# Gated delta rule on one Trainium2 core: solves of four heads, three chains at a time, and a new order of the products

## The chip, the cores and the metric

The kernel runs on one core of one Trainium2 chip. The metric is the time of one execution on the device in microseconds, as the median of three runs. A core has five engines that run side by side, each through its own list of instructions in order: TensorE (PE, matrix products), VectorE (DVE), ScalarE (ACT), GpSimd (POOL) and SyncE (SP), which here only issues DMA transfers. An instruction that needs another engine's result waits for a semaphore, and everything behind it in its engine's list waits with it.

## What is computed

One launch computes two residual blocks and a feed-forward part over 512 tokens of width 1024, batch 1, all in fp32. The first block adds two mixers, a gated delta rule of eight heads (width 128, chunks of 64 tokens in the reference) and a causal attention (MLA) of eight heads; then come a gated feed-forward part with a short convolution, and a second block (a state-space mixer beside a short convolution). The change touches only the delta rule:

```python
def gdn_chunked(q, k, v, g, beta):
    ...
    lmat = jnp.einsum("bhnid,bhnjd->bhnij", k_beta, k) * decay
    rhs = jnp.concatenate([v_beta, k_beta * jnp.exp(g)[..., None]], axis=-1)
    sol = lax.linalg.triangular_solve(lmat, rhs, left_side=True, lower=True, unit_diagonal=True)
    ...
    def step(state, inp):
        u_n, w_n, qd_n, kd_n, a_n, gl_n = inp
        v_new = u_n - jnp.einsum("bhck,bhkv->bhcv", w_n, state)
        o = jnp.einsum("bhck,bhkv->bhcv", qd_n, state) + jnp.einsum("bhij,bhjv->bhiv", a_n, v_new)
        state = state * gl_n[..., None, None] + jnp.einsum("bhck,bhcv->bhkv", kd_n, v_new)
        return state, o
    s0 = jnp.zeros((b, h, dk, dv), dtype=f32)
    _, o = lax.scan(step, s0, xs)
```

A unit lower triangular matrix is inverted for each chunk and head, and then a state of 128 x 128 runs through the chunks of a head, one after the other.

## The kernel before

The program is written by a generator in Python. Its bulk is a long row of linears: for each, eight blocks of weights of 128 x 128 are multiplied with activations of 512 tokens. An fp32 product is made of three fast ones (hi by hi, hi by lo, lo by hi), where `hi` is a rounded copy and `lo` the rest. The weights lie in memory in the order in which they are used, in chunks of eight blocks (512 KB). SP loads a chunk into one of two `raw` tiles (`NRAW`), ACT writes its `hi`, and DVE or POOL its `lo`, each into one of three tiles (`NHL`). A linear that belongs to the delta rule or to the attention is followed by work on its outcome.

That work is split into small tasks, Python generators that yield what they need next. `Emit.drive` (line 466) asks every running task for its next piece, and a planner (`Timeline`, with a cost for each instruction) tells which of them can go first; that one's instructions are written out. The main task is the row of linears, and it goes through `GDN_ORDER` (lines 31 to 36), a table written by hand; `order` (line 103) packs the weights by the same table. `kq` stands for the k and q of a head, `vg` for its v and output gate, `brb` and `bra` for the two gates of the block, `low`, `att`, `wv` and `ya` for the attention and the projections of both mixers. `LIMIT` (line 225) says how many tasks of one class may run at once, and `room()` counts free tiles of a common pool of 72 (`NG`), which are given back when nothing in Python refers to them any more. Since every instruction is issued by one helper, all rows of the profile read L243, and tiles tell them apart.

The tasks of a head:

- `t_gdn_a` (class a, two at once) normalises k and q, makes the matrices `ln` (the triangular one, four chunks of 128 tokens) and `at`, and sends the 32 x 32 blocks on the diagonal of `ln` to DRAM (`ldram`). After every second head it starts a solve.
- `t_solve` (class solve, one at once) loads the blocks of `NSOLVE` heads (line 1961) as `sl`, one block in each of 16 partitions a head, and inverts them in `sx`, in 31 steps of a multiplication into `st` and an addition into `sx`. For every four steps `idle` picks DVE or POOL by what the planner takes for their load. The inverses go to DRAM (`xdram`).
- `t_gdn_b` (class b, two at once) loads the inverses of its head as `X`, turns v, and completes the inverses of 128 x 128 with four groups of small products of 64 rows; `yodd`, one of two tiles, chosen by whether the head is odd, is an operand of the second. Then it runs the chain over four chunks: `gr` (from the state `gst`), `gvn` (from the inverse `Y`), and the next `gst`. Each is a product on PE and one instruction on DVE that reads it. Last come a norm and the gate.

```python
        for j0 in range(0, 31, 4):
            eng = self.idle(4000, 2000, POOL_BIAS)
```

Names that stand in rows: `mm` and `pt` are the results of products in PSUM (`mm` those of linears), `v` a convolution over the outcome of a linear (also for q and k, under their names), `rq_u` a step of an inverse square root.

Of the kernel before, what the change touches and what calls it, by code (L numbers as in the profile page):

```python
# [27 lines left out]


START = ["ab", ("k", 0), ("q", 0), ("k", 1)]  # L30
GDN_ORDER = [("kq", 3), ("vg", 0), ("brb", 0), ("kq", 4), ("brb", 1), ("vg", 1), ("brb", 2), ("vg", 2), ("brb",
             3), ("brb", 4), ("brb", 5), ("vg", 3), ("kq", 5), ("brb", 6), ("kq", 6), ("vg", 4), ("kq", 7),
             ("brb", 7), ("vg", 5), ("vg", 6), ("low",), ("vg", 7), ("bra", 0), ("wv", 0), ("bra", 1), ("bra",
             2), ("att", 0), ("att", 1), ("bra", 3), ("bra", 4), ("bra", 5), ("bra", 6), ("bra", 7), ("ya", 0),
             ("att", 2), ("ya", 1), ("att", 3), ("ya", 2), ("att", 4), ("wv", 1), ("ya", 3), ("att", 5), ("ya",
             4), ("att", 6), ("ya", 5), ("att", 7), ("ya", 6), ("ya", 7)]
PAIR_FFN = 3
FOLD_FFN = 3
# [64 lines left out]
def order():  # L103
# [5 lines left out]
    o = [START] + one([("q", 1), ("k", 2), ("q", 2)])  # L109
    for item in GDN_ORDER:  # L110
        if item[0] == "kq":
# [110 lines left out]
NHL = 3  # L222
AHEAD = 2
ROOM = {"kq": 5, "vg": 8, "att": 6, "wv": 5}
LIMIT = {"a": 2, "b": 2, "att": 2, "ssd": 2, "solve": 1, "E": 1, "pv": 1}


LAT = {"DVE": 33, "ACT": 33, "PE": 53, "POOL": 78, "SP": 60}
# [165 lines left out]
class Emit:  # L394
# [47 lines left out]
    def spawn(self, gen, cls=None):  # L442
        t = dict(gen=gen, cls=cls, need=None)
        if cls is not None and sum(x["cls"] == cls for x in self.tasks) >= LIMIT[cls]:
            self.waiting.setdefault(cls, []).append(t)
# [353 lines left out]
    def setup(self):  # L799
        nc, a = self.nc, self.a  # L800
        self.params = self.const.tile([128, NPARAM], F32, name="params")
        self.sqc = sq = self.const.tile([128, 5 * 128], F32, name="sqc")
        v = [sq[:, 128 * i:128 * i + 128] for i in range(5)]
        self.ident, self.ones, self.upper, low32, neg = v
        self.diag32 = low32[0:64, 0:64]
        self.yodd = []
        for i in range(2):
            t = self.const.tile([64, 256], F32, name=f"yodd{i}")
            nc.gpsimd.memset(t, 0.0)
            self.yodd.append(t)  # L810
        self.neg = neg

        self.rq, self.nk, self.bk = (self.const.tile([128, 32], F32, name=n) for n in ("rq", "nk", "bk"))
        self.ldram = self.dr.tile([8, NC, 4, 32, 32], F32, name="ldram")
        self.xdram = self.dr.tile([8, NC, 4, 32, 32], F32, name="xdram")
        one = self.s(1, "one", bufs=1)
        nc.gpsimd.memset(one, 1.0)
        nc.scalar.activation(one, one, AF.Silu)

        z = self.g(BF16, "warm")  # L820
        nc.vector.memset(z, 0.0)
        p = self.pt()
        for _ in range(NWARM):
            self.MM(p, z[:, 0:128], z, start=True, stop=True)
        self.hd, self.E = {}, {}
        self.oa, self.ob = {}, {}
# [121 lines left out]
    def t_gdn_a(self, h, kq):  # L948
        nc = self.nc
        hs = slice(4 * h, 4 * h + 4)  # L950
        yield self.flag("gates")

        yield lambda: "k" in kq
        k = kq["k"]
        yield [k]
        ss = self.s(8, "ss")
        pk = self.transpose4(k)
        junk = self.g(name="junk")
        yield [pk]
        for c in range(NC):  # L960
            nc.scalar.activation(junk[:, self.cc(c)], pk[:, self.cc(c)], AF.Square, accum_out=ss[:, c:c + 1])
        yield lambda: "q" in kq
        q = kq["q"]
        yield [q]
        pq = self.transpose4(q)
        yield [pq]
        for c in range(NC):
            nc.scalar.activation(junk[:, self.cc(c)], pq[:, self.cc(c)], AF.Square, accum_out=ss[:, 4 + c:5 + c])
        yield [ss]
        nc.vector.tensor_scalar(ss, ss, EPS, None, ALU.add)  # L970
        r = yield from self.rsqrt(ss, 8, "rkq")
        col = self.s(8, "kcol")
        nc.vector.tensor_tensor(col[:, 0:4], self.kdec[:, hs], r[:, 0:4], ALU.mult)
        del junk
        kt = self.g(name="ktok")
        nc.vector.tensor_tensor(self.v4(kt), self.v4(pk), self.colbc(col[:, 0:4]), ALU.mult)
        nc.vector.tensor_copy(self.rq[:, hs], r[:, 4:8])
        nc.vector.tensor_tensor(self.nk[:, hs], ss[:, 0:4], r[:, 0:4], ALU.mult)
        nc.vector.tensor_tensor(self.bk[:, hs], self.cmp[:, 64 + 4 * h:68 + 4 * h], r[:, 0:4], ALU.mult)
        nc.vector.scalar_tensor_tensor(col[:, 4:8], self.bk[:, hs], -1.0, r[:, 0:4], ALU.mult, ALU.mult)  # L980
        yield lambda: h in self.E
        e = self.E.pop(h)
        egb = self.rowload(self.grow[1, h])
        yield [e]
        at = self.g(name="at")
        ln = self.g(name="ln")
        for t, x, f in ((ln, k, col[:, 4:8]), (at, q, r[:, 0:4])):
            p = self.mm4(k, x)
            yield [p]
            for c in range(NC):  # L990
                nc.vector.scalar_tensor_tensor(t[:, self.cc(c)], p[:, self.cc(c)], f[:, c:c + 1], e[:, self.cc(c)],
                                               ALU.mult, ALU.mult)
        yield [ln]
        for b in range(4):
            nc.sync.dma_start(
                self.ldram[h, :, b].rearrange("c j i -> j c i"),
                self.v4(ln)[32 * b:32 * b + 32, :, 32 * b:32 * b + 32])
        yield [egb]
        nc.gpsimd.tensor_tensor(q, q, egb, ALU.mult)
        self.hd[h] = dict(kd=kt, kT=k, ln=ln, at=at, qd=q)  # L1000
        if h % NSOLVE == NSOLVE - 1:
            self.spawn(self.t_solve(h - NSOLVE + 1, NSOLVE), "solve")

    def t_solve(self, h0, n):

# [26 lines left out]
    def t_gdn_b(self, h, vg):  # L1032
# [3 lines left out]
        d = self.hd.pop(h)  # L1036
# [3 lines left out]
        X = self.g(name="X")  # L1040
        nc.gpsimd.memset(X, 0.0)

        ln = d["ln"]
        T = self.g(name="T")
        lnodd = T[:, 256:512].rearrange("p (c i) -> p c i", c=NC)
        nc.scalar.copy(T[:, 256:512].rearrange("p (c a i) -> p c a i", c=NC, a=2),
# [4 lines left out]
                self.v4(X)[32 * b:32 * b + 32, :, 32 * b:32 * b + 32],  # L1051
                self.xdram[h, :, b].rearrange("c i j -> i c j"))
        yield lambda: "v" in vg
        v = vg["v"]
        yield [v]
        p = self.transpose4(v)
        vb = self.g(name="vb")
        yield [p]
        nc.vector.tensor_tensor(self.v4(vb), self.v4(p), self.colbc(self.nk[:, hs]), ALU.mult)
# [10 lines left out]
        p = self.pt()  # L1070
        for c in range(NC):
            self.MM(half(p)[0:64, c], lnodd[:, c], xe[:, c, :, 0], start=True, stop=True)
        Yo = self.yodd[h % 2]
        for a in range(2):
            nc.vector.transpose(q4(Yo)[side(a), :, a], xe[odd(a), :, a, 1])
        yield [p]
# [3 lines left out]
        p = self.pt()  # L1080
        for c in range(NC):
            self.MM(half(p)[0:64, c], half(Yo)[:, c], half(T)[0:64, c], start=True, stop=True)
        yield [p]
        for a in range(2):
            nc.vector.tensor_copy(xe[odd(a), :, a, 0], q4(p)[side(a), :, a])
        for a in range(2):
            o, i = slice(64 * a + 32, 64 * a + 64), slice(64 * a, 64 * a + 32)
# [4 lines left out]
        for c in range(NC):  # L1092
            self.MM(half(p)[64:128, c], self.v4(ln)[0:64, c, 64:128], self.v4(X)[0:64, c, 0:64],
                    start=True, stop=True)
        yield [p]
        nc.scalar.copy(T[64:128, :256], p[64:128, :256])
        yield [T, Y]
# [49 lines left out]
        a = self.s(4, "soa")  # L1147
# [192 lines left out]
    def block1(self):  # L1340
# [95 lines left out]
        yield from self.unfold()  # L1436
        for item in GDN_ORDER:
            if item[0] == "kq":
# [184 lines left out]
    def t_dt(self, w, xh, fold):  # L1623
# [15 lines left out]
        p = self.pt()  # L1639
        for c in range(NC):  # L1640
            self.nc.tensor.transpose(p[:, 32 * c:32 * c + 32], z[0:32, self.cc(c)], self.ident[0:32, 0:32])
        pt = self.s(64, "dtr", bufs=1)
        yield [p]
        nc.vector.tensor_reduce(pt, p[:, 0:128].rearrange("p (c j q) -> p c q j", c=NC, j=2), AX.X, ALU.add)
        pt = self.v4(pt)
# [312 lines left out]
        yield from self.block2()  # L1958


NSOLVE = 2
SLACK = 0
POOL_BIAS = 2200
NWARM = 10
# [44 lines left out]
```

## Time and profile before

| what | value |
|---|---|
| median of three runs | 1508.0 us (1507.99 to 1508.04) |
| the profiled execution | 1510.79 us |
| its span, first to last instruction | 1508.8 us |
| PE busy | 1461.3 us, 97% |
| DVE, ACT, POOL busy | 887.0, 662.9, 553.5 us |
| mean granted clock of TensorE | 0.985 |

The page of the profile gives busy times over the whole program. The delta rule stands in its first third, so the windows of the trace (busy time of each engine in a stretch) and the chain of instructions in that third say more than the page's shares. In a row, a duration in brackets with an arrow is the idle time of the engine ahead of that instruction, and whose work ended it.

### The profile page before, as it was taken

How to read it: one execution, taken by the hardware profiler on the slowest of the kernel's cores; microseconds unless marked ns; L12 is line 12 of the kernel's file. 1: busy time of each engine (PE TensorE's matmuls, PEld its weight loads, DVE VectorE, ACT ScalarE, POOL GpSimd, SP SyncE). 2: the span in 40 equal slices, each digit the busy share in tenths (PEclk: the TensorE clock that was granted, in tenths of full speed). 3: DMA queues.
4: the chain of work that ended last, by engine and by line, in shares of the span. 5: the costliest groups of instructions: out<-in, count | busy, mean ns of one | idle time of the engine just before them, and what ended most of it. 6: DMA issues, size and time to landing. Idle time of an engine off the chain costs nothing.

```text
span 1508.8 us, 19107 instructions
## 1 busy us (share of the span) xinstructions
PE 1461.3 (97%) x7084; PEld 1196.9 (79%) x7084; DVE 887.0 (59%) x1801; ACT 662.9 (44%) x1124; POOL 553.5 (37%) x365
## 2 busy tenths in 40 slices
PE   8699989999999999999999999999999999999998
PEld 6588777787888888888888888888787787878877
DVE  7979978888854555348542044434975574360073
ACT  4565344433455655345442144344454453442342
POOL 0211124314143333442655455544115434543421
PEclk9899999999999999999999999999999999999999
DMA  5144413232231223442333332332233434422322
GB/s 185 53 121 138 122 46 93 79 97 64 70 95 60 63 78 105 147 126 84 111 99 98 97 97 89 95 103 94 70 95 114 122 98 119 125 87 89 95 94 98
DMA packets 56957, 147.63 MB, mean 98 GB/s; under 512 B 15072, under 2 KB 15648, under 8 KB 56864
## 3 DMA queue, kind: packets, MB, share of 16 engines
q1 hardware_dynamic: 56864, 146.42, 32.0%
q8 instruction: 55, 0.90, 0.2%
q14 instruction: 38, 0.31, 0.1%
HBM read 139.48 MB, written 5.34 MB: 96 GB/s over the span
## 4 chain that ended last, share of the span: by engine, by line
PE 59%; DVE 3%; issue 0%; ACT 0%; POOL 0%; DMA 0%; DVEq 0%; ACTq 0%
PE mm L243 56%; PE pt L243 3%; DVE lo L243 1%; DVE mix L243 0%; DVE xr L243 0%; DVE xbc L243 0%; DVE ysc L243 0%; DMA raw<-wstream 0%; DVE xn L243 0%; ACT hi L243 0%; DVE ms_a L243 0%; DVE sh L243 0%; POOL sh L243 0%; POOL xn L243 0%; POOL rs L243 0%
## 5 line engine op out<-in xcount | busy, mean ns | idle before, releaser
L243 PE MATMUL mm<-hi,hi 128*128 128x512 f32 (+2 forms) x1872 | 748.5, 400 | 6.5 <-ACT hi L243 4.4
L243 PE MATMUL mm<-lo,hi 128*128 128x512 f32 (+2 forms) x1872 | 731.9, 391 | 10.7 <-DVE lo L243 10.7
L243 PE MATMUL mm<-hi,lo 128*128 128x512 f32 (+2 forms) x1872 | 730.6, 391 | 3.7 <-DVE lo L243 3.7
L243 POOL TENSOR_TENSOR lo<-raw,hi 128x1024 fp32r<-128x1024 f32 x149 | 358.2, 2404 | 542.2 <-ACT hi L243 500.5
L243 PEld LDWEIGHTS mm<-lo,hi 128*128 128x128 f32 x1872 | 356.3, 190 | 79.0 <-DVE lo L243 13.1
L243 PEld LDWEIGHTS mm<-hi,lo 128*128 128x128 f32 x1872 | 355.2, 190 | 79.8 <-DVE lo L243 5.1
L243 PEld LDWEIGHTS mm<-hi,hi 128*128 128x128 f32 x1872 | 355.6, 190 | 78.8 <-ACT hi L243 8.5
L243 ACT ACTIVATE hi<-raw 128x1024 fp32r<-128x1024 f32 (+1 forms) x230 | 242.3, 1053 | 250.9 <-PE mm L243 175.6
L243 DVE TENSOR_TENSOR lo<-raw,hi 128x1024 fp32r<-128x1024 f32 (+1 forms) x81 | 100.2, 1238 | 2.8 <-ACT hi L243 2.7
L243 DVE TENSOR_TENSOR sq<-sq,sq 128x512 f32<-128x512 f32 x43 | 32.7, 773 | 93.1 <-ACT sq L243 92.9
L243 DVE TENSOR_TENSOR xr<-xr,mm 128x512 f32<-128x512 f32 x24 | 16.5, 687 | 97.5 <-PE mm L243 97.5
L243 DVE TENSOR_TENSOR lo<-fu,hi 128x512 fp32r<-128x512 f32 x22 | 44.6, 2027 | 42.0 <-ACT hi L243 42.0
L243 DVE SCALAR_TENSOR_TENSOR fu<-mm,params,fu 128x510 f32<-128x510 f32 (+1 forms) x38 | 28.5, 749 | 61.5 <-ACT fu L243 60.9
L243 ACT ACT_TABLE_LOAD x43 | 55.2, 1283 | 11.1 <-DVE k L243 2.2
L243 POOL TENSOR_TENSOR st<-sl,sx 32x112 f32<-32x112 f32 (+15 forms) x47 | 24.0, 512 | 80.2 <-issue 34.2
L243 POOL TENSOR_TENSOR fu<-fg,fu 128x512 f32<-128x512 f32 x22 | 30.0, 1361 | 42.4 <-DVE fu L243 42.4
L243 POOL TENSOR_TENSOR q<-q,row 128x512 f32<-128x512 f32 x8 | 10.9, 1365 | 78.7 <-PE pt L243 73.9
L243 DVE TENSOR_TENSOR lo<-scz,hi 128x512 fp32r<-128x512 f32 x8 | 15.8, 1969 | 32.7 <-ACT hi L243 32.7
L243 DVE TENSOR_TENSOR lo<-pt,hi 128x512 fp32r<-128x512 f32 (+3 forms) x32 | 15.7, 489 | 31.4 <-ACT hi L243 31.3
L243 DVE TENSOR_TENSOR st<-sl,sx 32x247 f32<-32x247 f32 (+15 forms) x77 | 29.9, 388 | 4.8 <-POOL sx L243 2.6
L243 DVE SCALAR_TENSOR_TENSOR fg<-mm,params,fg 128x510 f32<-128x510 f32 (+1 forms) x38 | 28.2, 743 | 6.2 <-ACT fg L243 5.5
L243 ACT ACTIVATE fg<-fg 128x512 f32<-128x512 f32 x22 | 13.9, 632 | 40.4 <-DVE fg L243 40.3
(314 smaller groups left out, 1578.8 us busy)
## 6 DMA issues: line engine op xcount, KB each, us to landing
raw<-wstream SPq DMA_DIRECT2D x228, 512.0 KB, 3.6
row<-grow_d SPq DMA_DIRECT2D x16, 256.0 KB, 4.2
row<-crow_d SPq DMA_DIRECT2D x16, 256.0 KB, 4.5
x<-xT SPq DMA_DIRECT2D x8, 256.0 KB, 6.5
sbd<-gate SPq DMA_DIRECT2D x8, 256.0 KB, 2.0
sb<-sbd SPq DMA_DIRECT2D x8, 256.0 KB, 3.8
xr<-xT SPq DMA_DIRECT2D x8, 256.0 KB, 3.8
Ce<-crow_d SPq DMA_DIRECT2D x16, 128.0 KB, 4.7
```

The source lines that it names most:

```text
L243: return f(*args, **kw)
```

## The change

Solves are made of four heads at a time on 64 partitions: two solves of 31 steps in place of four. A solve starts when all its heads have sent their blocks. Three chains may run at once, each with a `yodd` tile of its own, taken from a list and given back. A head's `ln` and `v` are dropped from the dictionaries that held them, so that their tiles come free once they are used. A tile of the second block shares the buffer of another (`gyb`). The table of the linears is new: it starts with a gate (`brb` 0) and the v of head 0, and the heads' k and q come earlier against their v.

```diff
@@ -28,11 +28,11 @@
-GDN_ORDER = [("kq", 3), ("vg", 0), ("brb", 0), ("kq", 4), ("brb", 1), ("vg", 1), ("brb", 2), ("vg", 2), ("brb",
...
+GDN_ORDER = [("brb", 0), ("vg", 0), ("kq", 3), ("brb", 1), ("brb", 2), ("kq", 4), ("brb", 3), ("brb", 4), ("brb",
...
@@ -222,7 +222,7 @@
 ROOM = {"kq": 5, "vg": 8, "att": 6, "wv": 5}
-LIMIT = {"a": 2, "b": 2, "att": 2, "ssd": 2, "solve": 1, "E": 1, "pv": 1}
+LIMIT = {"a": 2, "b": 3, "att": 2, "ssd": 2, "solve": 1, "E": 1, "pv": 1}
@@ -804,7 +804,7 @@
         self.yodd = []
-        for i in range(2):
+        for i in range(LIMIT["b"]):
             t = self.const.tile([64, 256], F32, name=f"yodd{i}")
@@ -998,8 +998,10 @@
         self.hd[h] = dict(kd=kt, kT=k, ln=ln, at=at, qd=q)
-        if h % NSOLVE == NSOLVE - 1:
-            self.spawn(self.t_solve(h - NSOLVE + 1, NSOLVE), "solve")
+        self.flags.add(("L", h))
+        h0 = h - h % NSOLVE
+        if all(("L", i) in self.flags for i in range(h0, h0 + NSOLVE)):
+            self.spawn(self.t_solve(h0, NSOLVE), "solve")
@@ -1040,7 +1042,7 @@
-        ln = d["ln"]
+        ln = d.pop("ln")
         T = self.g(name="T")
@@ -1051,9 +1053,10 @@
         yield lambda: "v" in vg
-        v = vg["v"]
+        v = vg.pop("v")
         yield [v]
         p = self.transpose4(v)
+        del v
         vb = self.g(name="vb")
@@ -1070,7 +1073,7 @@
             self.MM(half(p)[0:64, c], lnodd[:, c], xe[:, c, :, 0], start=True, stop=True)
-        Yo = self.yodd[h % 2]
+        Yo = self.yodd.pop(0)
         for a in range(2):
@@ -1080,6 +1083,7 @@
             self.MM(half(p)[0:64, c], half(Yo)[:, c], half(T)[0:64, c], start=True, stop=True)
+        self.yodd.append(Yo)
         yield [p]
@@ -1092,6 +1096,7 @@
                     start=True, stop=True)
+        del ln
         yield [p]
@@ -1639,7 +1644,7 @@
             self.nc.tensor.transpose(p[:, 32 * c:32 * c + 32], z[0:32, self.cc(c)], self.ident[0:32, 0:32])
-        pt = self.s(64, "dtr", bufs=1)
+        pt = self.s(64, "gyb", bufs=1)
         yield [p]
@@ -1958,7 +1963,7 @@
-NSOLVE = 2
+NSOLVE = 4
 SLACK = 0
```

What it does to the lists of the engines, at three places. On DVE, where the first two chains begin (`st` and `sx` are steps of a solve, `gvn` and `gst` of the chains), the list before reads:

```order
L243 TENSOR_TENSOR st_1598<-sl_1519,sx_1520 32x256
L243 TENSOR_TENSOR sx_1520<-sx_1520,st_1598 32x16x16
L243 TENSOR_SCALAR gvn_1801<-pt_1799,bk 128x128
L243 TENSOR_SCALAR gvn_1804<-pt_1802,bk 128x128
...
L243 TENSOR_TENSOR lo_1843<-raw_1822,hi_1829 128x1024
L243 TENSOR_TENSOR st_1598<-sl_1519,sx_1520 32x255
L243 TENSOR_TENSOR sx_1520<-sx_1520,st_1598 32x15x17
...
L243 COPY gst_1850<-pt_1848 128x128
```

and after the change:

```order
L243 COPY Y_1706<-pt_1793 64x4x64
L243 TENSOR_SCALAR rkq_1779<-rq_t_1778 128x8
L243 TENSOR_TENSOR rq_u_1781<-rkq_1779 128x8
L243 TENSOR_TENSOR rq_u_1781<-rq_u_1781,rq_h_1780 128x8
L243 SCALAR_TENSOR_TENSOR rkq_1779<-rq_u_1781,rkq_1779 128x8
L243 TENSOR_SCALAR gvn_1808<-pt_1806,bk 128x128
L243 TENSOR_SCALAR gvn_1813<-pt_1811,bk 128x128
...
L243 COPY gst_1831<-pt_1829 128x128
L243 COPY gst_1835<-pt_1833 128x128
```

Before, the steps of the second solve (heads 2 and 3) stand between the steps of the chains of heads 0 and 1; now none does, since heads 0 to 3 have one solve that ends ahead of the chains. In their place stand the norms of the next heads' k and q.

On PE, with the change, where three chains run (heads 4 to 6; `mm` is a linear):

```order
L243 MATMUL pt_3316<-Y_3231,T_3176 64x64 x4
L243 MATMUL pt_3321<-gvn_3303,ktok_1631 128x128
L243 MATMUL pt_3324<-vb_3168,Y_3216 128x128
L243 MATMUL mm_3210<-hi_583,hi_3076 128x512
L243 MATMUL mm_3210<-lo_588,hi_3076 128x512
L243 MATMUL mm_3210<-hi_583,lo_3086 128x512
L243 MATMUL pt_3333<-gvn_3303,at_1639 128x128
L243 MATMUL pt_3336<-gvn_3326,ktok_1854 128x128
L243 MATMUL pt_3339<-vb_3187,Y_3231 128x128
L243 MATMUL pt_3344<-gst_3323,k_1230 128x128
```

Products of three heads stand between those of one linear; before, two heads were the most.

On SP, with the change, after the first solve:

```order
L243 DMA xdram<-sx_1203 64x1024
L243 DMA X_1612<-xdram 32x4x32 x4
L243 DMA row_1637<-grow_d 128x512
L243 DMA X_1647<-xdram 32x4x32 x4
L243 DMA ldram<-ln_1640 32x4x32 x4
L243 DMA row_1697<-grow_d 128x512
L243 DMA raw_1700<-wstream 128x1024
...
L243 DMA ldram<-ln_1863 32x4x32 x4
L243 DMA X_1955<-xdram 32x4x32 x4
L243 DMA raw_1964<-wstream 128x1024
```

The load of the weights `raw_1700` stands behind the store of the inverses, eight loads of inverses and the four stores of head 4's `ln`; `raw_1964` behind those of one head more.

## Rows read from the trace of the kernel before

**Rows 1.** The page's busy times (busy us, share, instructions).

```profile
PE 1461.3 (97%) x7084; PEld 1196.9 (79%) x7084; DVE 887.0 (59%) x1801; ACT 662.9 (44%) x1124; POOL 553.5 (37%) x365
```

**Rows 2.** Windows: start:end, length, busy PE PEld DVE ACT POOL, clock, DMA share, GB/s.

```profile
180.00:285.00 105.00, 94.20 (x543) 78.02 (x542) 85.19 (x257) 39.90 (x118) 41.66 (x71) 0.93 0.26 78
285.00:420.00 135.00, 132.16 (x751) 108.06 (x750) 114.77 (x312) 54.35 (x130) 30.92 (x28) 1.00 0.25 75
```

**Rows 3.** Timeline of PE, 173 to 200: start, us, operation, [idle before, releaser].

```profile
174.63 0.67 PE L243 MATMUL pt<-T,yodd 64*64 64x64 f32 x8
193.51 0.60 PE L243 MATMUL pt<-gvn,at 128*128 128x128 f32 x4
199.34 0.77 PE L243 MATMUL pt<-gst,k 128*128 128x128 f32 x2 [5.23 <-DVE gst L243]
```

**Rows 4.** Timeline of DVE, 173 to 200.

```profile
173.93 0.42 DVE L243 TENSOR_TENSOR T<-pt,sqc 64x256 f32<-64x256 f32 x1
188.23 0.40 DVE L243 TENSOR_TENSOR st<-sl,sx 32x247 f32<-32x247 f32 x1
191.67 0.59 DVE L243 TENSOR_SCALAR gvn<-pt,bk 128x128 f32<-128x128 f32 x2
195.53 0.40 DVE L243 TENSOR_TENSOR st<-sl,sx 32x255 f32<-32x255 f32 x1
198.93 0.47 DVE L243 COPY gst<-pt 128x128 f32<-128x128 f32 x2
```

**Rows 5.** Timeline of PE, 234 to 245.

```profile
238.63 1.11 PE L243 MATMUL pt<-T,yodd 64*64 64x64 f32 x8 [2.48 <-DVE T L243]
```

**Rows 6.** Windows of 5 us, columns as in rows 2.

```profile
200.00:205.00 5.00, 5.00 (x19) 4.19 (x19) 1.00 (x4) 1.44 (x2) 3.74 (x7) 0.55 0.02 5
240.00:245.00 5.00, 5.00 (x18) 3.56 (x17) 3.96 (x12) 0.28 (x1) 1.10 (x5) 0.50 0.57 166
```

**Rows 7.** Groups, 100 to 420: out<-in, shapes, count | busy, mean ns | idle.

```profile
L243 DVE TENSOR_TENSOR st<-sl,sx 32x247 f32<-32x247 f32 (+15 forms) x77 | 29.9, 388 | 4.8 <-POOL sx L243 2.6
L243 DVE TENSOR_TENSOR sx<-sx,st 32x247 f32<-32x247 f32 (+15 forms) x77 | 26.0, 338 | 2.7
L243 POOL TENSOR_TENSOR sx<-sx,st 32x112 f32<-32x112 f32 (+15 forms) x47 | 28.0, 595 | 3.7
L243 POOL TENSOR_TENSOR st<-sl,sx 32x112 f32<-32x112 f32 (+15 forms) x47 | 24.0, 512 | 80.2 <-issue 34.2 <-DVE rkq L243 29.1 <-DMA sl<-ldram 7.3
```

**Rows 8.** More groups of DVE, 100 to 420.

```profile
L243 DVE TENSOR_TENSOR lo<-raw,hi 128x1024 fp32r<-128x1024 f32 x31 | 38.2, 1233 | 0.0
L243 DVE SCALAR_TENSOR_TENSOR v<-mm,params,v 128x509 f32<-128x509 f32 (+2 forms) x21 | 15.6, 744 | 0.5
L243 DVE TENSOR_SCALAR gvn<-pt,bk 128x128 f32<-128x128 f32 x32 | 10.9, 343 | 5.2 <-PE pt L243 5.1
L243 DVE TENSOR_TENSOR rq_u<-rq_u,rq_h 128x4 f32<-128x4 f32 (+1 forms) x50 | 10.1, 204 | 1.1
```

**Rows 9.** The chain that ended last: start, us, engine, tile, instructions.

```profile
681.55 353.64 PE mm L243 x1560
1035.19 0.87 PE pt L243 x8
```

**Rows 10.** Timeline of PE, 270 to 283.

```profile
270.76 1.06 PE L243 MATMUL pt<-k 128*128 128x128 f32 x8
271.65 0.39 PE L243 MATMUL pt<-gst,k 128*128 128x128 f32 x2
```

**Rows 11.** Timeline of POOL and DVE, 358.5 to 362.5.

```profile
359.54 2.37 POOL L243 TENSOR_TENSOR lo<-raw,hi 128x1024 fp32r<-128x1024 f32 x1 [1.83 <-ACT hi L243]
359.60 2.35 DVE L243 TENSOR_SCALAR ms_a<-cs 128x4 f32<-128x4 f32 x1
```

**Rows 12.** SP's waits, 100 to 420 (us, times, longest); the page's landing times.

```profile
SPq L243 <- DVE ln L243: 13.7, 2, 8.2
raw<-wstream SPq DMA_DIRECT2D x228, 512.0 KB, 3.6
```

More of the change, by code (lines that the diff above doesn't have):

```diff
@@ L30 @@
 START = ["ab", ("k", 0), ("q", 0), ("k", 1)]
-GDN_ORDER = [("kq", 3), ("vg", 0), ("brb", 0), ("kq", 4), ("brb", 1), ("vg", 1), ("brb", 2), ("vg", 2), ("brb",
[L32 to L35, printed above, removed]
+GDN_ORDER = [("brb", 0), ("vg", 0), ("kq", 3), ("brb", 1), ("brb", 2), ("kq", 4), ("brb", 3), ("brb", 4), ("brb",
+             5), ("vg", 1), ("kq", 5), ("brb", 6), ("vg", 2), ("kq", 6), ("kq", 7), ("vg", 3), ("bra", 0),
+             ("brb", 7), ("vg", 4), ("vg", 5), ("vg", 6), ("low",), ("bra", 1), ("bra", 2), ("vg", 7), ("bra",
+             3), ("att", 0), ("wv", 0), ("att", 1), ("bra", 4), ("bra", 5), ("bra", 6), ("bra", 7), ("ya", 0),
+             ("att", 2), ("ya", 1), ("att", 3), ("wv", 1), ("ya", 2), ("att", 4), ("ya", 3), ("att", 5), ("ya",
              4), ("att", 6), ("ya", 5), ("att", 7), ("ya", 6), ("ya", 7)]
```

## The prediction

> **What bounds the kernel now.** I read the page's busy times first: PE is busy for 1461.3 us [rows 1], and DVE, the next, for 887.0. The change takes nothing from PE (6620 instructions in its list before and after, the same products in another order), so it can gain only what PE stands idle or runs slowly. Next come the windows of the stretch that the change reorders. In 180 to 285 PE is busy for 94.2 of 105 us, in 285 to 420 for 132.16 of 135 [rows 2]: it is idle for 10.8 + 2.8 = 13.6 us. In the first of these windows DVE is busy for 85.19 us, and the clock that TensorE was granted is 0.93. The timeline then tells where the idle time is: the longest wait is one of 5.23 us for `gst`, the first state of a chain [rows 3], the next one of 2.48 us for `T` in a later head [rows 5]. Behind each the granted clock falls, to 0.55 and 0.50 in five microseconds [rows 6], that is, for part of that time it stood on the lower of its levels, 1.2 GHz in place of 2.4. The cost is 0.45 x 5 + 0.5 x 5 = 4.75 us of PE's time. So the stretch loses 13.6 + 4.75 = 18.35 us, and that is the most that a better order can give back.
>
> **Why PE waits there.** From the end of the row `T` of head 1, at 173.93 + 0.41, to the first `gst`'s successor on PE at 199.34 DVE works 25.0 us without a gap; PE has products from 174.63 to 194.11, 19.5 us, and then nothing that does not need DVE [rows 3, 4]. 25.0 less 19.5 is 5.5, the wait. Of the 58 rows of DVE in it, counted from `T`, 32 are steps of the solve of heads 2 and 3. Sixteen of them run from 188.23 to 191.67 and from 195.53 to 198.93, 6.84 us [rows 4], straight ahead of `gvn` and of `gst`; the others by the means, (388 + 338) / 2 = 363 ns [rows 7], 5.8 us; together 12.6 us. The wait is thus made by a solve that DVE does between the steps of two chains.
>
> **The change, part by part.**
>
> Solves of four heads. A step on 64 partitions in place of 32 has as many elements in each partition; I take its time as unchanged, since the bound from above, twice the time, would need DVE to go by partitions, and a convolution of 128 partitions and 509 elements takes 744 ns, a solve's step of 32 partitions and at most 256 takes 388 on the mean [rows 7, 8]. In the list DVE has 54 + 54 steps in place of 77 + 77, POOL 8 + 8 in place of 47 + 47. On DVE that takes away 23 x (0.388 + 0.338) = 16.7 us; on POOL 39 pairs of 0.51 + 0.60 us by the means [rows 7], 43 us, which nobody waited for there. Half of the 124 pairs are gone altogether. What hides the 16.7 us of DVE now is PE's own work wherever DVE isn't late; so it counts only where PE waits.
>
> The first two chains. In the list after the change no step of a solve stands between their steps, but the solve's end comes later against the heads, and other rows have taken the place. From the convolutions of the next k to the `gr` of the second chunk the list of DVE has 81 rows: 6 convolutions, 6 more of 512 elements, 29 of at most 8 elements, 2 `lo`, 38 of 128 or 256. By the means that is 12 x 0.744 + 29 x 0.204 + 2 x 1.233 + 38 x 0.343 = 8.9 + 5.9 + 2.5 + 13.0 = 30.3 us [rows 8]. Means count some time twice, since instructions overlap at their ends: the 26 rows of before without the solve would make 4 x 1.233 + 3 x 0.744 + 19 x 0.343 = 13.7, and took 25.4 - 12.6 = 12.8, a share of 0.935. So I take 28.3 us. PE has, between the same two points, 53 products of linears at 353.64 / 1560 = 0.227, 16 transposes at 0.87 / 8 = 0.11 [rows 9], 24 products of 128 x 128 at (271.65 - 270.76) / 4 = 0.22 [rows 10] and 32 of 64 rows at 0.67 / 4 = 0.17 [rows 3]: 12.0 + 1.8 + 5.3 + 5.4 = 24.5 us. PE is short by 28.3 - 24.5 = 3.8 us, which I take as the wait in place of 5.23. From below it is nothing, if the planner's list runs as it thinks; from above 30.3 - 24.5 = 5.8, the means as they are.
>
> Three chains at once. Where heads 4 to 6 run, the list has 67 rows of DVE, some 23 us by the same prices, against 48 products of linears and as many of the chains, 28 us. DVE is not late there. Before, two chains leave less of other work between a product of a chain and the next; a third fills it. The price of the third `yodd` is one memset at the start, beside loads; the taking and giving back of these tiles and of `ln` and `v` issues nothing. The rename in the second block has no instruction.
>
> The other waits. Without the two longest 13.6 - 5.23 - 2.48 = 5.9 us are left in small pieces, each for a row that DVE does late. With 16.7 us less on DVE I take half, 2.9 us; all of it and nothing are the bounds. The 2.48 us I take as gone: the place in the order where they stood no longer exists; if it stays, it costs 2.5 and another 2.5 of clock.
>
> The clock. After 5.23 and 2.48 us of waiting it was granted at about half for five microseconds [rows 6]. A wait of 3.8 us in one piece would cost some 2.4, in short pieces perhaps nothing; I take half of the 2.5, 1.25. By the section "HAM oscillation" of the Trainium skill's page "TensorE: Matmul & The Clock Gate", pauses of PE between bursts of products bring the slow clock back again and again; the two rows agree that a pause is followed by it. By that rule alone, with each pause punished, the term would be 2.5, and the sum 1.25 more.
>
> SP. The loads of weights stand behind more transfers than before. A load lands in 3.6 us [rows 12], and both halves need at most 2 x 1.233 more [rows 8]: 6.1 us. Between the time at which `raw_1700` may be written and its first product PE has 48 products of linears (10.9 us) and by the same prices 11.8 us of the heads' own: 22.7 us. Less 6.1 and the two landings of the inverses' way through DRAM, 7.2, that leaves 9.4 us. I cost it at nothing.
>
> Sum: 3.8 + 2.9 + 1.25 = 8.0 us of loss in place of 18.35, a gain of 10.4. The profiled execution took 1510.8 us, 2.8 above the median of the three runs, and becomes 1500.4; the median becomes 1508.0 - 10.4 = **1497.6**.
>
> **The rivals.**
>
> *All waits go* (chance 0.12). The loss is nothing, the gain 18.35, the time 1489.6. For it speaks that DVE is also slowed by what POOL does: a row on four elements took 2.35 us beside a `lo` of POOL of 2.37 that had begun just before it [rows 11], where such a row takes 0.2 [rows 8]. With 43 us less of two-operand work on POOL such holds become rarer, and the planner, which knows none of them, is nearer to the truth. Against it: the 149 `lo` of POOL all stay, and DVE's row sum of the first chains is above PE's. The Trainium skill, "SBUF — State Buffer", section "SBUF: two separate sides", states that DVE and GpSimd share a pair of ports as a lock that one holds for a whole instruction; the row agrees.
>
> *Three chains bind each other* (0.12). A chain has its DVE row between any two of its products. With three at once 30 such rows of `gvn`, `gr` and `gst` (ten in each) at 0.343 [rows 8] could each stand ahead of a product that another chain needs: 10.3 us, the time 1497.6 + 10.3 = 1507.9, no change. Against it: PE has more work there than DVE, 28 against 23 us.
>
> *The weights come late* (0.08), the one on the other side. SP waits in order: the four stores of a `ln` wait for DVE, and `raw_1700` stands behind them, `raw_1964` behind the next. Before, SP waited up to 8.2 us for a `ln` [rows 12]. It decides when SP is held for over 9.4 us there. Two such waits, 16.4 us, at each of the two places make PE wait 7.0 us and cost 2.25 of clock: 18.5 us, the time 1516.1. Against it: before, no wait of PE in this stretch was for weights behind such a row.
>
> **How the numbers follow.** My forecast has 0.68. Its own range is from 1508.0 - 18.35 + 2.9 = 1492.5 (no wait in the first chains, no clock) to 1497.6 + 2.0 + 3.0 + 1.25 = 1503.9 (5.8 us there, all small waits, the whole clock term). With the first rival, 0.80 lie from 1489.6 to 1503.9; since prices are uncertain by a microsecond or two, and the second rival may come at part of its strength, I give 1488 to 1506. A measurement tells 0.2%, 3 us, from no change. Faster than 1505.0: forecast and first rival, 0.80. Within 3 us: the second rival, 0.12. Slower: the third, 0.08.
>
> **What would show it.** Right: 54 steps of each kind on DVE between 100 and 420, with about the same means, on 64 partitions; no step of a solve in the 25 us ahead of the first `gst`; PE's longest wait below 4 us and for a `gr`, `gvn` or `gst`; idle time of PE in the stretch at 6 to 7 us, and at most one window of 5 us with a clock near 0.5. The rest of the program, from the end of the attention on, the same to a microsecond. Wrong: a wait of PE for `hi` or `lo` behind an SP that waits for `ln`, steps of 64 partitions that take much longer than 0.36 us, waits for `gvn` and `gst` many and short where three chains run, or a changed time after 420.

## The result

The kernel after the change took 1485.1 us (median of four runs, 1484.6 to 1488.2) against 1508.0 of the kernel before: 0.985 of its time, 95% interval 0.9835 to 0.9869. That is 22.9 us less where 10.4 were forecast, and 2.9 us below the range. The sign was right, the size was not. The profiled execution took 1485.2 us with a span of 1483.2, so 25.6 us of span are gone; that of before stood 2.8 us above its median, that of after only 0.1.

The page's busy times after the change, which answer to [rows 1]:

```profile
PE 1449.1 (98%) x7084; PEld 1191.0 (80%) x7084; DVE 864.5 (58%) x1755; ACT 655.1 (44%) x1118; POOL 503.9 (34%) x284
```

PE has the same 7084 records and is busy for 12.2 us less, and idle for 1483.2 - 1449.1 = 34.1 us in place of 47.5, 13.4 less. Where the idle time went is seen in the windows, with the columns of [rows 2]; the third stretch, which the prediction did not look at, is shown for both kernels, after first:

```profile
180.00:285.00 105.00, 104.53 (x628) 86.68 (x627) 86.55 (x260) 46.58 (x131) 16.86 (x21) 1.00 0.31 94
285.00:420.00 135.00, 133.76 (x770) 111.22 (x769) 108.79 (x305) 59.33 (x134) 19.14 (x10) 1.00 0.25 74
420.00:600.00 180.00, 180.00 (x910) 153.22 (x909) 91.57 (x213) 98.55 (x198) 69.98 (x34) 1.00 0.30 90
```

```profile
420.00:600.00 180.00, 177.84 (x902) 150.13 (x901) 96.94 (x224) 104.65 (x215) 67.45 (x33) 1.00 0.27 83
```

In the three stretches PE is idle for 0.5, 1.2 and 0 us; before it was 10.8, 2.8 and 2.2. The granted clock is at its upper level in all three. Ahead of them nothing is gained: after the change PE is idle for 1.2 us between 100 and 180, where it was never idle before, and in the first 100 us it is idle for 0.9 us less, at a mean clock of 0.86 in place of 0.90.

PE's largest waits between 100 and 600 after the change (us, times, longest):

```profile
PE pt L243 <- DVE X L243: 0.9, 2, 0.6
PE pt L243 <- POOL q L243: 0.8, 1, 0.8
PE pt L243 <- ACT k L243: 0.4, 1, 0.4
PE pt L243 <- DVE gst L243: 0.3, 1, 0.3
```

No wait for a chain's `gvn` or `gr` is left, and one of 0.3 us for `gst`, where 5.23 stood in [rows 3]. From 600 on the program is as before with one exception. In the second block PE waits for a tile `dtz` as before, but in the kernel before the clock fell behind that wait, and after the change it did not (the wait and a window of 5 us, before, then after):

```profile
1080.70 0.43 PE L243 MATMUL pt<-sqc,dtz 32*128 32x32 f32 x4 [2.27 <-DVE dtz L243]
1080.00:1085.00 5.00, 4.30 (x14) 3.41 (x15) 4.93 (x8) 1.35 (x2) 0.00 (x0) 0.67 0.00 0
```

```profile
1056.30 0.43 PE L243 MATMUL pt<-sqc,dtz 32*128 32x32 f32 x4 [2.25 <-DVE dtz L243]
1055.00:1060.00 5.00, 3.70 (x18) 3.06 (x19) 4.93 (x8) 0.76 (x2) 0.00 (x0) 1.00 0.01 2
```

That is some 1.6 us of the 25.6, and it may be part of the 2.8 us by which the profiled execution of before stands above its median. The one edit in the second block, the shared buffer, does not decide it: the wait is 2.25 to 2.27 us long in the profiles of both kernels and of all twelve experiments below, and the clock falls behind it in ten of the fourteen. Of the four without the fall, two share that buffer (after, e12) and two do not (e8, e10).

The solves are what the list said. The groups of DVE, 100 to 420, after the change, which answer to [rows 7], with one size of step by its own shape, and that size before:

```profile
L243 DVE TENSOR_TENSOR st<-sl,sx 64x135 f32<-64x135 f32 (+15 forms) x54 | 23.2, 429 | 5.2 <-POOL sx L243 3.8
L243 DVE TENSOR_TENSOR sx<-sx,st 64x135 f32<-64x135 f32 (+15 forms) x54 | 18.9, 350 | 1.9
...
L243 DVE TENSOR_TENSOR st<-sl,sx 64x252 f32<-64x252 f32 x4 | 1.7, 414 | 0.1
```

```profile
L243 DVE TENSOR_TENSOR st<-sl,sx 32x252 f32<-32x252 f32 x6 | 2.5, 409 | 0.2
```

54 steps of each kind, and one on 64 partitions takes 414 ns where one on 32 takes 409: twice the heads at the same price. DVE has 13.8 us less of them than before (42.1 in place of 55.9), where the prediction took 16.7 by the means.

### The profile page after: what moved, and what is told of

Its sections match the earlier page's. It is cut to its first block, busy times and chain, and to the rows that moved or that the text cites. A ratio compares the mean times of both kernels' runs of the same rounds, so it can differ in the third digit from the quotient of the medians.

```text
span 1483.2 us, 18958 instructions
## 1 busy us (share of the span) xinstructions
PE 1449.1 (98%) x7084; PEld 1191.0 (80%) x7084; DVE 864.5 (58%) x1755; ACT 655.1 (44%) x1118; POOL 503.9 (34%) x284
## 4 chain that ended last, share of the span: by engine, by line
PE 85%; DVE 10%; DMA 2%; issue 1%; POOL 1%; ACT 1%; SPq 0%; DVEq 0%; POOLq 0%; ACTq 0%
PE mm L243 76%; PE pt L243 9%; DVE lo L243 3%; DVE st L243 1%; DVE sx L243 1%; DVE k L243 0%; DVE q L243 0%; SPq L243 0%; DVE rq_u L243 0%; DVE mix L243 0%; DMA raw<-wstream 0%; DVE v L243 0%; DVE xr L243 0%; DVE x L243 0%; ACT hi L243 0%
## 5 line engine op out<-in xcount | busy, mean ns | idle before, releaser
L243 POOL TENSOR_TENSOR q<-q,row 128x512 f32<-128x512 f32 x8 | 10.4, 1294 | 157.9 <-PE pt L243 92.5
L243 ACT ACT_TABLE_LOAD x37 | 47.5, 1283 | 8.3 <-DVE xbc L243 2.6
L243 DVE TENSOR_TENSOR lo<-pt,hi 128x512 fp32r<-128x512 f32 (+3 forms) x32 | 15.6, 489 | 28.9 <-ACT hi L243 28.8
L243 DVE SCALAR_TENSOR_TENSOR fg<-mm,params,fg 128x510 f32<-128x510 f32 (+1 forms) x38 | 28.3, 744 | 6.2 <-ACT fg L243 5.5
L243 POOL TENSOR_TENSOR xdd<-xd,dd 128x512 f32<-128x512 f32 x8 | 9.4, 1176 | 58.7 <-DVE xd L243 58.6
L243 DVE TENSOR_SCALAR row<-row,cmp 128x128 f32<-128x128 f32 x64 | 26.9, 487 | 0.0
(314 smaller groups left out, 1513.9 us busy)
```

The lines of the kernel that those rows point to most:

```text
L243: return f(*args, **kw)
```

## The experiments

Times are medians; the ratio is to the kernel before, on the same chips, with its 95% interval. The kernel after the change is 0.985 [0.9835, 0.9869].

| run | what | us | ratio |
|---|---|---|---|
| e1 | after, solves of two | 1529.5 | 1.014 [1.013, 1.016] |
| e2 | after, two chains | 1491.9 | 0.990 [0.988, 0.992] |
| e3 | before, solves of four | 1513.9 | 1.004 [1.003, 1.006] |
| e4 | after, old table | 1507.2 | 0.999 [0.998, 1.000] |
| e5 | after, tiles kept | 1509.6 | 1.001 [1.000, 1.002] |
| e6 | before, new table | 1549.7 | 1.028 [1.025, 1.030] |
| e7 | e4, solves on DVE | 1508.0 | 0.999 [0.998, 1.001] |
| e8 | before, second solve on POOL | 1502.5 | 0.996 [0.995, 0.997] |
| e9 | after, 8 tiles asked | 1504.9 | 0.998 [0.997, 0.999] |
| e10 | before, tiles given back | 1508.8 | 1.001 [1.000, 1.002] |
| e11 | after, 71 tiles | 1498.7 | 0.993 [0.992, 0.995] |
| e12 | after, other table | 1489.9 | 0.989 [0.987, 0.991] |

### Did the solve's steps make the long wait?

e8 takes the steps of the second solve off DVE in the kernel before and changes nothing else.

```diff
-            eng = self.idle(4000, 2000, POOL_BIAS)
+            eng = nc.gpsimd if h0 == 2 else self.idle(4000, 2000, POOL_BIAS)
```

> The kernel before the change with the second solve (heads 2 and 3) on POOL altogether, so that DVE has no step of it between the steps of the first two chains. If those steps made the wait of 5.23 us, as the prediction said, it is gone or under 1 us, and with it the first fall of the clock: 1499 to 1503 us, unless heads 2 and 3 now wait for their X. If the wait came from a lack of other products there, PE waits 4 us or more for gst or gvn as before, and the time is 1506 to 1512 us.

The stretch of the first two chains, 180 to 200, in the kernel before and then in e8 (columns of [rows 2]):

```profile
180.00:200.00 20.00, 14.47 (x88) 11.29 (x87) 18.35 (x42) 6.56 (x14) 0.79 (x2) 0.94 0.39 118
```

```profile
180.00:200.00 20.00, 20.00 (x117) 17.43 (x117) 11.47 (x29) 8.13 (x25) 17.87 (x28) 1.00 0.13 41
```

PE is busy for all of the 20 us in place of 14.47, DVE for 11.5 in place of 18.4. That part of the prediction is shown: the steps between those of the chains made the wait. The whole is 5.3 us faster, in the range expected. PE comes to head 2 sooner in return and waits 2.6 us there, for a `T` by the profile; the inverses of heads 2 and 3 are themselves stored earlier (at 202.8 in place of 212.6).

e1 does the opposite and puts solves of two back into the kernel after.

```diff
-NSOLVE = 4
+NSOLVE = 2
```

> The kernel after the change with NSOLVE = 2 alone set back (new table, three chains, tiles given back early all kept). In its list DVE has steps of the second solve between the first chain's gvn, gst and gr again. Theory A (the gain comes from solves that no longer stand between the steps of the chains): a wait of PE for gst or gr of 5 us or more is back, the clock falls behind it, and the time is 1497 us or more. Theory B (the gain comes from the table of the linears and the third chain, which give PE other work meanwhile): PE's waits between 100 and 420 stay under 5 us together and the time is within 5 us of 1485.

Timeline of PE in e1, and of DVE ahead of that wait (eight steps lie from the first to the last row but one):

```profile
195.11 0.56 PE L243 MATMUL pt<-gvn,at 128*128 128x128 f32 x2 [4.57 <-DVE gst L243]
```

```profile
187.93 0.39 DVE L243 TENSOR_TENSOR st<-sl,sx 32x247 f32<-32x247 f32 x1
...
191.02 0.41 DVE L243 TENSOR_TENSOR sx<-sx,st 32x256 f32<-32x256 f32 x1
...
194.97 0.28 DVE L243 COPY gst<-pt 128x128 f32<-128x128 f32 x1
```

The wait for `gst` is back with 4.57 us; 3.5 us of solve steps stand ahead of it on DVE, and behind them 3.3 us of convolutions and a `lo`. Another of 5.1 for `gvn` comes later, and PE is idle for 28.8 us between 100 and 600. Theory A of the expectation holds in kind, though the wait for `gst` is just under its 5 us. The time goes further: with the rest of the change in place, solves of two are 21 us worse than the kernel before.

### Which part carries the gain?

e3 takes the solves of four alone, e6 the table alone, both in the kernel before; e4 is the kernel after with the old table.

```diff
-NSOLVE = 2
+NSOLVE = 4
```

> The kernel before the change with NSOLVE = 4 alone (old table, two chains, tiles kept). Its list has no step of a solve on DVE between the steps of the first chains. Theory A: the waits of 5.2 and 2.5 us and the two falls of the clock go, 13 us or more are gained, the time is 1495 us or less. Theory B: the chains start later, after all of four heads, without the table that makes room for it, and the time is 1503 to 1512 us.

The edit of e6 (that of e4 is its reverse, in the kernel after):

```diff
-GDN_ORDER = [("kq", 3), ("vg", 0), ("brb", 0), ("kq", 4), ("brb", 1), ("vg", 1), ("brb", 2), ("vg", 2), ("brb",
...
+GDN_ORDER = [("brb", 0), ("vg", 0), ("kq", 3), ("brb", 1), ("brb", 2), ("kq", 4), ("brb", 3), ("brb", 4), ("brb",
...
```

> The kernel before the change with the new GDN_ORDER alone (solves of two, two chains, tiles kept). Theory C (table and solve of four only pay together, the third chain is worth 7 us by itself): 1529.5 us of the run with solves of two plus about 7, 1532 to 1540 us, with waits for gvn and gst behind solve steps. Theory B (the table gives PE other work in any case): 1500 us or less.

> The kernel after the change with the old GDN_ORDER (solves of four, three chains and early tiles kept). Theory A: no solve between the steps of the chains, so the time stays at 1485 to 1491 us. Theory B: without the new table most of the gain is lost, 1497 us or more.

e3 ended above both ranges, at 1513.9. No wait for `gst` is left and only 0.8 us for a `T`, as its theory A said, but others have come. PE's longest between 100 and 600 in e3:

```profile
PE pt L243 <- ACT hi L243: 6.5, 2, 5.6
PE pt L243 <- DMA X<-xdram: 4.5, 1, 4.5
```

In e3 the planner also gave 46 of the 62 pairs of steps to POOL (8 in the kernel after), so it does not tell the size of the solve from the engine that makes it; it was not repeated with the steps on DVE. e6 is the worst of all, 1549.7, 10 us beyond what I expected of the worse theory, and its longest wait, 8.7 us, is for an `X`, not for `gvn` or `gst`: neither edit brings anything alone. e4 answers for B, 1507.2: without the table the rest of the change is worth nothing. In e4 PE waits for the inverse itself, and late in the last chains (timeline of PE):

```profile
185.90 1.08 PE L243 MATMUL pt<-X,T 128*64 128x64 f32 x8 [4.06 <-DMA X<-xdram]
...
382.52 0.49 PE L243 MATMUL pt<-gst,k 128*128 128x128 f32 x2 [0.59 <-DVE gst L243]
384.35 0.46 PE L243 MATMUL pt<-gr,Y 128*128 128x128 f32 x2 [1.34 <-DVE sof L243]
...
387.43 1.09 PE L243 MATMUL pt<-sqc,X 128*128 128x128 f32 x4 [1.27 <-ACT T L243]
```

From 379.8 to 388.9 there is no product of a linear between these rows: PE has only the chain of the head that is left, and stands between its steps. The first of the rows could have another reason: with the old table the planner gave 39 of 62 steps to POOL, where a pair takes longer. e7 tests it, with the old table as in e4.

```diff
-            eng = self.idle(4000, 2000, POOL_BIAS)
+            eng = nc.vector if j0 else nc.gpsimd
```

> The kernel after the change with the old table, and with the solves put on the engines that they have after the change (the first four steps on POOL, the others on DVE) where the planner had chosen POOL for 39 pairs of 62. Theory D (with the old table the inverses come late because POOL makes them): the wait of 4.1 us for X near 181 is gone, and the time is 1497 us or less. Theory C (the old table has too little other work for PE while any solve of four heads runs, and DVE is late with the k, q and v of the next heads instead): waits of 5 us or more stay between 180 and 420, and the time is 1502 us or more.

The wait for X went, as D said, and the time stayed at 1508.0, as C said: in its place came waits of 2.7 us for `gst` at 240 and 2.7 for a tile `sq` at 329, and the short ones near 385 stand in both (5.1 us in four pieces in e7). D falls. C's single wait of 5 us did not come, and its reason, that DVE is late with the next heads, was not tried.

e2 takes the third chain away.

```diff
-LIMIT = {"a": 2, "b": 3, "att": 2, "ssd": 2, "solve": 1, "E": 1, "pv": 1}
+LIMIT = {"a": 2, "b": 2, "att": 2, "ssd": 2, "solve": 1, "E": 1, "pv": 1}
```

> The kernel after the change with LIMIT of class b set back to 2 (two chains at once, two yodd tiles), the rest kept. Theory A (solves out of the way): the first chains' part of DVE's list is as with three, so no wait over 2 us there, and the time is 1485 to 1489 us. Theory B (table and third chain): with two chains PE has too little between the steps of a chain, waits for gvn, gr and gst come back in many short pieces, and the time is 1493 us or more.

PE's two longest waits between 100 and 600 in e2:

```profile
PE pt L243 <- DVE gr L243: 2.8, 1, 2.8
PE pt L243 <- DVE ln L243: 1.6, 1, 1.6
```

1491.9 lies between the two theories: the third chain is worth 6.9 us, and what comes back without it is above all one wait of 2.8 for a `gr` and one of 1.6, not many short ones. Eight pairs of steps more are on POOL in e2, by the planner's choice.

### The tiles that I had costed at nothing

e5 leaves `ln` and `v` in their dictionaries.

```diff
-        ln = d.pop("ln")
+        ln = d["ln"]
...
-        v = vg.pop("v")
+        v = vg["v"]
...
-        del v
...
-        del ln
```

> The kernel after the change, but a head's ln and v stay in their dictionaries as before, so their tiles come free later. The list of DVE is the same up to the end of the first chains; then the planner chooses otherwise (33 steps of a kind on DVE and 33 on POOL in place of 54 and 8). Theory A (giving back early costs and brings nothing by itself): 1483 to 1488 us. Theory B (it makes room for the third chain): X tiles come late, PE waits for X or T between 285 and 420, and the time is 1490 us or more.

1509.6 us: two references held longer take all of the gain away. In the trace the planner has also put 31 pairs of steps on each of DVE and POOL, in place of 54 and 8. e9 asks how the tiles act, without keeping one.

```diff
-ROOM = {"kq": 5, "vg": 8, "att": 6, "wv": 5}
+ROOM = {"kq": 8, "vg": 8, "att": 6, "wv": 5}
```

> The kernel after the change with one number altered: the linears of a head's k and q now start only when 8 tiles of the common pool are free, in place of 5 (ROOM, kq). Nothing is computed otherwise, and ln and v are still given back early. Theory E (the early giving back matters since it lets the linear of head 6's k start while head 2's inverse is completed; without free tiles PE has no linear to put between the small products): the wait for room is the same one as in the run with kept tiles, PE stands between the small products at 210 to 217, 7 to 8 us are lost by the 650th weight product, and the time is 1492 to 1510 us. Rival (kept tiles cost by themselves, by writes that wait for old readers): no such waits, the time within 3 us of 1485.

The timeline of PE in e9 while the inverse of head 2 is completed:

```profile
208.69 0.39 PE L243 MATMUL mm<-hi,lo 128*128 128x512 f32 x1
208.92 0.38 PE L243 MATMUL pt<-gst,q 128*128 128x128 f32 x2
210.29 0.49 PE L243 MATMUL pt<-gvn,at 128*128 128x128 f32 x2 [0.99 <-DVE gvn L243]
210.71 0.67 PE L243 MATMUL pt<-T,yodd 64*64 64x64 f32 x8
211.80 0.67 PE L243 MATMUL pt<-X,ln 64*64 64x64 f32 x8 [0.41 <-DVE X L243]
212.93 0.68 PE L243 MATMUL pt<-Y,T 64*64 64x64 f32 x8 [0.46 <-DVE soa L243]
214.82 0.80 PE L243 MATMUL pt<-vb,Y 128*128 128x128 f32 x2 [1.22 <-DVE Y L243]
215.93 1.09 PE L243 MATMUL pt<-sqc,X 128*128 128x128 f32 x4 [0.31 <-PE pt L243]
```

and after the change, at the same place:

```profile
209.74 0.39 PE L243 MATMUL mm<-hi,lo 128*128 128x512 f32 x1
209.97 0.40 PE L243 MATMUL mm<-hi,hi 128*128 128x512 f32 x1
...
211.35 0.38 PE L243 MATMUL pt<-gst,q 128*128 128x128 f32 x2
...
211.88 0.68 PE L243 MATMUL pt<-T,yodd 64*64 64x64 f32 x8
212.49 0.50 PE L243 MATMUL mm<-hi,hi 128*128 128x512 f32 x1
...
216.11 0.68 PE L243 MATMUL pt<-X,ln 64*64 64x64 f32 x8
...
217.61 0.68 PE L243 MATMUL pt<-Y,T 64*64 64x64 f32 x8
```

Until 209 both do the same, e9 some 1 us earlier. After the change the linear of the next head's k begins at 209.97, and its products fill the time between `T,yodd`, `X,ln` and `Y,T`. In e9 that linear is not in the list yet, since it asks for 8 free tiles; nothing else was altered, and e5's timeline has the same waits at the same place; the small products stand one behind the other, each waiting for what DVE makes of the one before. Between the 600th and the 650th product of a linear e9 loses 7.9 us against the kernel after, and by the 2000th, after the second set of chains, 21. Theory E holds for the first 7.9, and e9's 1504.9 lies in its range. The other 13 come between 285 and 600 and are not shown to be such a wait for room: in e9, as in e5, 31 pairs of steps are on POOL in place of 8, and PE's longest wait, 3.5 us at 312, is for an `X`. The clock adds to the first 7.9, by the windows of 5 us in e9:

```profile
210.00:215.00 5.00, 2.62 (x27) 2.09 (x28) 4.47 (x27) 1.96 (x5) 0.00 (x0) 0.94 0.00 0
215.00:220.00 5.00, 4.69 (x16) 3.94 (x17) 4.16 (x15) 0.54 (x3) 0.00 (x0) 0.50 0.02 5
```

e10 gives the same tiles back in the kernel before.

```diff
-        ln = d["ln"]
+        ln = d.pop("ln")
...
-        v = vg["v"]
+        v = vg.pop("v")
...
+        del v
...
+        del ln
```

> The kernel before the change with ln and v given back early alone (old table, solves of two, two chains). Theory E: with two chains and solves of two the pool has room when a linear wants to start, so giving back brings nothing by itself: 1505 to 1512 us. Rival (the giving back is what makes the gain, whatever the table): 1497 us or less.

1508.8, no gain: the tiles are worth nothing where the waits come from solve steps (a wait for `gst` of 5.3 us is still there). e11 undoes the shared buffer of the second block, by which the third `yodd` fits beside 72 tiles.

```diff
-        pt = self.s(64, "gyb", bufs=1)
+        pt = self.s(64, "dtr", bufs=1)
...
-NG = 72
+NG = 71
```

> The kernel after the change with the shared buffer of the second block undone: dtr has its own buffer again, and since the memory of a partition is then too small for 72 tiles and a third yodd, the common pool has 71 tiles (NG). Theory E (the change stands or falls with free tiles): the run is as after the change up to the last chains, to about 400 us; there the linear of the attention's second head asks for 6 tiles and gets them later, PE has only small products of the last head meanwhile, and the time is 1489 to 1500 us. Rival (one tile of 72 is nothing): 1484 to 1487 us.

Windows of e11 and of the kernel after, and e11's wait in the first:

```profile
410.00:420.00 10.00, 4.79 (x25) 3.87 (x24) 8.41 (x32) 6.92 (x16) 0.86 (x1) 0.91 0.00 0
```

```profile
410.00:420.00 10.00, 10.00 (x50) 8.38 (x50) 8.07 (x30) 8.27 (x19) 2.80 (x1) 1.00 0.23 67
```

```profile
416.55 0.33 PE L243 MATMUL pt<-sqc,P 128*128 128x128 f32 x1 [3.54 <-ACT P L243]
```

Up to the 1200th product of a linear, at 394, e11 keeps the lag of 0.6 to 1.1 us that it has from the start. Then the last head and the attention's first stand alone, PE is busy for 4.8 of 10 us, and the clock is lower until 430 (0.92 in 420 to 430). By the 1300th product 6.7 us are lost there; by the 1600th it is 11.1, with four short waits for `hi` near 500 that the kernel after does not have. One tile of 72 is worth 13.6 us of median.

### A version that beats both?

```diff
-GDN_ORDER = [("brb", 0), ("vg", 0), ("kq", 3), ("brb", 1), ("brb", 2), ("kq", 4), ("brb", 3), ("brb", 4), ("brb",
-             5), ("vg", 1), ("kq", 5), ("brb", 6), ("vg", 2), ("kq", 6), ("kq", 7), ("vg", 3), ("bra", 0),
...
+GDN_ORDER = [('kq', 3), ('brb', 0), ('vg', 0), ('brb', 1), ('brb', 2), ('kq', 4), ('brb', 3), ('brb', 4), 
+             ('brb', 5), ('vg', 1), ('kq', 5), ('vg', 2), ('brb', 6), ('kq', 7), ('vg', 3), ('kq', 6), 
...
```

> The kernel after the change with eight neighbours or near neighbours of GDN_ORDER exchanged (kq 3 first, vg 2 ahead of brb 6, kq 7 and vg 3 ahead of kq 6, vg 5 ahead of vg 4, and four later ones). The generator's planner puts the end of the attention 1.4 us earlier with it. Theory E (72 tiles are just enough and PE's waits between 100 and 600 are down to 3 us, so a table can give little more): 1482 to 1488 us. Rival (the list is on an edge, and a table that gives three chains to heads 0 to 2 as well moves a solve to POOL and brings waits back): 1490 us or more.

1489.9 us (0.989 [0.987, 0.991]) is outside E's range and a hair below the rival's bound: faster than before and no better than the change. Its six executions spread from 1485.8 to 1497.3, those of the change from 1484.6 to 1488.2, and the profile is of one that took 1487.0. In it 35 pairs of steps are on POOL, as the rival said, and 7.7 us of idle time stand between 100 and 600, the longest wait 2.5 us for X from DRAM. The 1.4 us that the planner saw were not found on the chip.

## Why the prediction was right and wrong

**Where it failed.** Two steps of the sum failed: the ceiling of 18.35 us, and the loss of 8.0 us that was kept below it, above all the 3.8 us of the first two chains. By the windows, the idle time of 180 to 420 went from 13.6 to 1.7 us, and both falls of the clock went (4.75): 16.6 of the 18.35 came back, 6.3 more than forecast (3.8 of the first chains, 1.25 of the clock, 1.2 of the small waits). The other 9.0 us of the 25.6 lie outside the ceiling, and more than half of them has no assigned cause. The prediction's own sign of being wrong, a changed time after 420, came.

**The cause of the waits: right.** The 5.23 us come from a solve between the steps of two chains (e8, e1), no step of it is left in front of `gvn` and `gst` (the last one ends 22 us ahead of the first `gst`), and a step on 64 partitions costs what one on 32 does.

**The first two chains, 3.8 us: mis-sized, it is 0.** The 81 rows of DVE were taken at 28.3 us, by means times 0.935. They took 26.2 (timeline of DVE after the change, from the first convolution to the end of `gr`, then the window of just this stretch):

```profile
167.97 2.30 DVE L243 SCALAR_TENSOR_TENSOR k<-mm,params,k 128x509 f32<-128x509 f32 x3
...
193.52 0.60 DVE L243 SCALAR_TENSOR_TENSOR gr<-pt,neg_eg,vb 128x128 f32<-128x128 f32 x2
```

```profile
167.97:194.12 26.15, 25.28 (x182) 20.70 (x181) 24.87 (x83) 11.43 (x35) 1.68 (x2) 1.00 0.37 109
```

DVE is busy for 24.87 us of it and PE for 25.28, where the prediction had 28.3 and 24.5: there is no shortfall, and PE's one wait there, 0.8 us, is for POOL's `q`. The share 0.935 came from a stretch without rows of a few elements, and such rows can overlap more (three of some 0.15 us begin 0.07 apart at 173.2).

**The small waits, 2.9 us: too large, it is 1.7.** In 180 to 420, the stretch that the term was made for, 0.5 + 1.2 us of idle time are left. The 1.2 us between 100 and 180 are new and belong to no term. The wait of 2.48 us is gone, as taken.

**The clock, 1.25 us: it is 0.** No fall is left in this stretch. That short pieces perhaps cost nothing cannot be relied on, though: in e9 the clock fell among waits of 0.99, 0.41, 0.46, 1.22 and 0.31 us, to 0.50. For another kernel the Trainium skill states that frequent short pauses of PE between groups of products make the clock swing between its two levels ("TensorE: Matmul & The Clock Gate", section "A second HAM failure mode: psum-queue depth-cycling"); e9's windows agree.

**"The most that a better order can give back", 18.35 us: wrong.** It was idle time of two windows and two falls of the clock. Left out were 2.2 us between 420 and 600, where the last chains meet the attention, and the 1.6 us in the second block, which come and go. The 0.9 us less before 100 are offset by the 1.2 more between 100 and 180. Of the 12.2 us by which PE's busy time fell, the 1.6 and the two falls (4.75) explain 6.4. The other 5.8, or more, since the clock of the first 100 us is lower after the change, are not assigned: products that start late by less than a shown wait may be a part, and no run shows it.

**Giving back tiles "issues nothing": true, but no measure of its worth.** I costed instructions, and the price of these edits is in the order that the generator writes. Without them (e5) the change is worth nothing, and one tile is worth 13.6 us (e11). This did not move the number: the sum was made on the finished list, in which all of it was already paid. It made the account of the parts wrong.

**The rivals.** All waits gone, 1489.6, was nearest, and the time is still 4.5 us below it: 1.7 us of idle time remain in its stretch, so its condition holds nearly, and the rest came from outside. Whether POOL's smaller share had a part in it was not tried. Three chains that bind each other did not come; the third chain is a gain of 6.9 us (e2). Weights late behind SP did not come: PE waits for no `hi` or `lo` there.

**Open.** Why the table and the solves of four pay only together is shown by their results (e1, e3, e4, e6) and, for the old table, by PE without linears at 380; which entries of the table do it was not tried, and neither was the third chain alone in the kernel before. That a solve of four needs other linears beside it is argued. In e2, e3, e4, e5, e9 and e12 the planner also gave more steps of the solves to POOL than in the kernel after; only e7 takes this away, for e4.

## What to carry to other kernels

Where a generator or scheduler places work by what is free, a reference that is held too long can be a cost on the critical path: count free tiles at each point where a large piece asks for them, and try one tile less before believing that an edit costs nothing. Here the first tile less already cost 13.6 us; 70 and 73 tiles were not tried. Parts of a change to an order have no prices of their own: solves of four, the table and the tiles each brought nothing or a loss when put into the kernel before by themselves, and with a third chain 23 us together.

## What the runs showed that I had not expected

A step of a solve on DVE costs the same for 64 partitions as for 32 (414 and 409 ns), so the larger batch was free. Among five short waits in a row, of 0.3 to 1.2 us, the clock fell as deep (0.50) as behind one of 2.5. And one wait of 2.25 to 2.27 us in the second block, the same in all fourteen profiles, cost the clock in ten of them (0.67 in the kernel before) and not in four (1.00 in the kernel after): 1.6 us may come and go with no edit near.
